# Latent attention: score rows of 640 keys split as 384 + 256 columns, and one query copy on ScalarE

## The chip, the cores and the metric

The kernel runs on one core of a Trainium2 chip. The metric is the device time of one execution in microseconds (us). An execution that the hardware profiler recorded shows for every engine when each instruction began and how long it took. The engines are TensorE (PE, with its weight loads as PEld), VectorE (DVE), ScalarE (ACT), GpSimd (POOL) and SyncE (SP, which here only issues DMAs). Each takes its instructions in the order of the program and waits on semaphores for the others.

## The reference

A trunk of two layers over 1024 tokens of width 1024: differential attention, then multi-head latent attention, each followed by a gated MLP with a short causal convolution; RMSNorm before each. The change touches the latent attention alone, which computes for 16 heads

```python
q = (c_q @ w_uq).reshape(b, s, 16, 64 + 32)           # 64 plain, 32 rotary
kv = (c_kv @ w_ukv).reshape(b, s, 16, 64 + 64)        # keys, values
sc = (q_nope . k_nope + q_pe . k_pe) * scale
p = softmax(where(key_chunk <= query_chunk, sc, -max))  # chunks of 64 tokens
o = p @ v
```

A block of 128 queries sees its own and all earlier keys, so query block i (0 to 7) needs (i + 1) x 128 columns of scores.

## The kernel before

Matmuls run in a rounded 32-bit format, three for one product: every operand is kept as a high part (a copy into that format) and a low part (the rest), and `mm3` adds high x low, high x high and low x high. Its three calls stand in the profile as lines L120, L121 and L122. High parts are made by `hi` (L126 when it goes to DVE, L128 on ACT), low parts by `lo` (L131, on DVE or POOL).

One step of the attention (`MlaStep`) takes one head and two neighbouring query blocks, j = 0 and 1:

- `scores(j)`: `mm3` into a tile S of PSUM (1024 columns, two banks; there are two such tiles, used in turn, so a score row can begin only when the row before the last has been read out). A matmul writes at most 512 columns, so a row is cut by `blocks(n)` into 512 and the rest. Then DVE writes the mask into a corner (L2017) and takes the row's maximum (L2018), and ACT takes the exponential with its sum (L2019; the sum is read out by a second ACT instruction on the same line), which frees the tile.
- `weigh(j)`: DVE inverts the sum (L2025), POOL scales the row (L150).
- `turn`: PE transposes the weighted rows by 128 columns into a bank b (L264; three banks in turn, shared with the projections of queries and keys), ACT and DVE make high and low parts of it, tiles u.
- `product`: those by the values, on L2039 and L2040; ACT and DVE add up the two halves (L2042, L2043) and ACT's queue stores them (L2045).

A row of 640 keys is query block i = 4: step p = 2, j = 0, once a head, 16 times in all. In `scores` the row begins at column 0 of its tile:

```python
sc, e = k.big()[:, :n], self.e[:, :n] if n > 512 else ...
for b, m in blocks(n):
    k.mm3(sc[:, b : b + m], q[:, 0, qs], ...)
```

Between the steps, the projections of the next pair of heads are woven in: `q_unit` projects 512 tokens of one head's queries by nine matmuls into a bank, DVE multiplies by the rotary table (L1720, into a tile h), and the high and low parts go into a tile s. Which engine makes each part is read from strings with one letter per call (S for ACT, V for DVE, P for POOL): `QUERIES` for the high and `QUERIES_LOW` for the low parts, at place 2 x head + half.

The order on each engine is not that of the code. A scheduler keeps the dependencies and, with its own estimates, chooses at each point what an engine issues next; only the differential attention has an order written by hand. So an edit of one instruction can move others after it.

Of the kernel before, what the change touches and what calls it, by code (L numbers as in the profile page):

```python
# [18 lines left out]
P = 128  # L19
# [21 lines left out]
def blocks(n, step=512):  # L41
    return [(a, min(step, n - a)) for a in range(0, n, step)]
# [14 lines left out]
class Trunk:  # L57
# [1608 lines left out]
    ROTARY = "SV"  # L1666
    VALUES = "SSVSSSSS"
    WEIGHTS = "SVSSSSSS"
    QUERIES = "SSSVSSSSSSSSSSSSSSSSSSSSSSSSSSSS"
    QUERIES_LOW = "VPPVPPVPPPPPPPPPPPPPPPPPPPPPPPPP"  # L1670
    KEYS = "SSSVSSSSSSSSSSSSSSSSSSSSSSSSSSSS"
    UNITS_AT = (2, 2, 3, 5, 5, 7)
# [1 line left out]
    def mla_heads(self, cT, v_d, o_d):  # L1674
# [33 lines left out]
        def q_unit(h, half):  # L1708
# [11 lines left out]
            nc.vector.tensor_mul(t, acc, cs[:, s])  # L1720
            self.hi(q[:, 0, s], t, eng(self.QUERIES[2 * h + half]))
            self.lo(q[:, 1, s], t, q[:, 0, s], eng(self.QUERIES_LOW[2 * h + half]))
# [106 lines left out]
class DaStep(Step):  # L1829
# [37 lines left out]
    def scores(self, j):  # L1867
        k, nc, hd = self.k, self.k.nc, self.hd
        i = 2 * self.p + j
        n = (i + 1) * P  # L1870
        q = hd["q"][i // 4]
        qs = slice((i % 4) * P, (i % 4 + 1) * P)
        sc = self.sc[j] = []
        for c in range(2):
            if c == 0 or not self.one:
                ps = k.big()
            sc.append(ps[:, c * 512 : c * 512 + n] if self.one else ps[:, :n])
        self.both[j] = ps.rearrange("p (c n) -> p c n", c=2)
        for b, m in blocks(n):
            kt = hd["k"][b // 512]  # L1880
            for x, (qp, kp) in enumerate(((1, 0), (0, 1), (0, 0))):
                for c in range(2):
                    rows = slice(64 * c, 64 * c + 64)
                    nc.tensor.matmul(sc[c][:, b : b + m], q[rows, qp, qs], kt[rows, kp, :m], start=x == 0, stop=x == 2)  # L1884
# [114 lines left out]
class MlaStep(Step):  # L1999
# [5 lines left out]
    def scores(self, j):  # L2005
        k, nc = self.k, self.k.nc
        i = 2 * self.p + j
        n = (i + 1) * P
        q, kt = self.hd["q"], self.hd["k"]
        qs = slice(i * P, (i + 1) * P)  # L2010
        nm, l = k.stat(), k.stat()
        if j == 0 or n > 512:
            self.e = self.R.P([P, S])
        sc, e = k.big()[:, :n], self.e[:, :n] if n > 512 else self.e[:, j * 512 : j * 512 + n]
        for b, m in blocks(n):
            k.mm3(sc[:, b : b + m], q[:, 0, qs], q[:, 1, qs], kt[:, 0, b : b + m], kt[:, 1, b : b + m], True, True)
        nc.vector.memset(sc[0:64, n - 64 : n], NEG)  # L2017
        nc.vector.tensor_reduce(nm, sc, axis=AX.X, op=ALU.max, negate=True)  # L2018
        nc.scalar.activation(e, sc, AF.Exp, bias=nm, accum_out=l)  # L2019
        self.l.append(l)  # L2020
        self.probs.append(e)
# [314 lines left out]
```

## Time and profile before

| | us |
|---|---|
| median of 3 runs (2372.78 to 2373.3) | 2373.1 |
| the profiled execution | 2372.74 |
| its span, first to last instruction | 2370.9 |
| PE busy | 2345.3 |
| DVE busy | 1919.9 |
| ACT busy | 1259.6 |
| POOL busy | 583.5 |

The granted clock of TensorE is 0.999. The latent attention's steps run from about 1285 to 1636 us of the span. A record of the timeline has start, length, engine, line, operation, output tile and input tiles with their sizes, and, in brackets, how long the engine was idle before it and what ended that. In the table of stretches a row has the stretch, its length, the busy time and count of PE, PEld, DVE, ACT and POOL, the granted clock, the DMA share and GB/s. A matmul's end is modelled, and matmuls overlap.

### The profile page before, as it was taken

The page shows a single profiled execution, that of the slowest core. Times are in us where ns is not written, and L with a number is a line of the kernel's source. Part 1 is how long each engine was busy: PE and PEld are TensorE (multiplying, and loading weights), DVE is VectorE, ACT ScalarE, POOL GpSimd, SP SyncE. Part 2 cuts the span into 40 slices and gives each one's busy share as a digit, 9 for nine tenths or more (in the row PEclk, how much of TensorE's full clock was granted, in tenths as well). Part 3 has the DMA queues.
Part 4 walks back from the last instruction along what each step waited for, and adds up shares of the span by engine and source line. Part 5 has one row for each costly group of instructions (what it writes and reads, how often), then busy time and mean ns, then how long its engine had stood idle before and what let it go on. Part 6 is the DMA issues. An engine that isn't in the chain of part 4 may idle for free.

```text
span 2370.9 us, 32976 instructions
## 1 busy us (share of the span) xinstructions
PE 2345.3 (99%) x12146; PEld 1976.2 (83%) x12146; DVE 1919.9 (81%) x3170; ACT 1259.6 (53%) x2315; POOL 583.5 (25%) x465
## 2 busy tenths in 40 slices
PE   9999999999999999999999999999999999999998
PEld 7888888788888888888898889988888888888886
DVE  6777878858888888999865888886588888889997
ACT  5666666745444444354444777775454444443444
POOL 4545444323000000000133666673420000000001
PEclk9999999999999999999999999999999999999999
DMA  3111111332222222652221211133322222227502
GB/s 148 40 36 36 49 37 54 111 134 94 89 80 81 80 89 80 234 174 86 84 99 56 72 33 39 41 98 110 114 79 88 80 80 83 87 80 284 178 1 80
DMA packets 95667, 213.42 MB, mean 90 GB/s; under 512 B 8713, under 2 KB 33937, under 8 KB 95505
## 3 DMA queue, kind: packets, MB, share of 16 engines
q1 hardware_dynamic: 86304, 183.51, 23.5%
q10 hardware_dynamic: 9200, 27.80, 3.2%
q8 instruction: 96, 1.57, 0.3%
q14 instruction: 67, 0.54, 0.1%
HBM read 158.85 MB, written 52.43 MB: 89 GB/s over the span
## 4 chain that ended last, share of the span: by engine, by line
PE 91%; DVE 5%; DMA 1%; ACT 1%; issue 1%; POOL 0%; POOLq 0%; DVEq 0%; SPq 0%; ACTq 0%
PE S L122 14%; PE S L120 14%; PE S L121 14%; PE b L120 9%; PE b L122 8%; PE b L121 8%; PE u L120 5%; PE u L122 5%; PE u L121 4%; PE S L1884 3%; PE b L264 2%; PE u L2040 1%; PE b L1930 1%; PE u L2039 1%; DVE s L131 1%
## 5 line engine op out<-in xcount | busy, mean ns | idle before, releaser
L168 POOL TENSOR_TENSOR st<-st,mhalf 128x1 f32<-128x1 f32 x56 | 35.3, 632 | 1296.1 <-DVE st L165 1287.4
L120 PE MATMUL S<-s,u 128*128 128x512 f32 (+1 forms) x800 | 301.8, 377 | 0.2 <-ACT u L1110 0.2
L122 PE MATMUL S<-s,u 128*128 128x512 f32 (+1 forms) x800 | 301.2, 376 | 0.1
L121 PE MATMUL S<-s,u 128*128 128x512 f32 (+1 forms) x800 | 301.0, 376 | 0.0
L128 ACT CAST u<-h 128x512 fp32r<-128x512 f32 (+1 forms) x194 | 115.8, 619 | 267.1 <-DVE h L1031 262.8
L120 PE MATMUL b<-s,u 128*128 128x512 f32 x588 | 230.8, 393 | 1.1 <-DVE u L131 0.4
L122 PE MATMUL b<-s,u 128*128 128x512 f32 x588 | 229.1, 390 | 0.0
L121 PE MATMUL b<-s,u 128*128 128x512 f32 x588 | 229.0, 389 | 0.0
L1088 DVE SCALAR_TENSOR_TENSOR u<-u,conv,u 128x1023 f32<-128x1023 f32 (+1 forms) x176 | 225.1, 1279 | 0.8 <-ACT u L1084 0.7
L150 POOL TENSOR_TENSOR u<-u,st 128x512 f32<-128x512 f32 (+7 forms) x160 | 173.1, 1090 | 161.1 <-DVE st L2025 107.3
L128 ACT CAST s<-u 128x512 fp32r<-128x512 f32 (+3 forms) x229 | 144.2, 663 | 100.2 <-PE u L122 28.7
L128 ACT CAST u<-b 128x512 fp32r<-128x512 f32 (+1 forms) x256 | 134.9, 547 | 92.1 <-PE b L1930 57.7
L131 DVE TENSOR_TENSOR u<-b,u 128x512 fp32r<-128x512 f32 (+1 forms) x256 | 158.6, 631 | 23.9 <-ACT u L128 22.8
L120 PEld LDWEIGHTS S<-s,u 128*128 128x128 f32 x800 | 150.6, 188 | 27.9 <-ACT u L1110 0.5
L122 PEld LDWEIGHTS S<-s,u 128*128 128x128 f32 x800 | 150.6, 188 | 27.8 <-DVE u L131 0.3
L121 PEld LDWEIGHTS S<-s,u 128*128 128x128 f32 x800 | 150.6, 188 | 27.4
L120 PE MATMUL u<-s,s 128*128 128x512 f32 (+1 forms) x408 | 165.1, 405 | 1.1 <-DVE s L131 0.9
L122 PE MATMUL u<-s,s 128*128 128x512 f32 (+1 forms) x408 | 158.3, 388 | 0.0
L121 PE MATMUL u<-s,s 128*128 128x512 f32 (+1 forms) x408 | 157.6, 386 | 0.0
L131 DVE TENSOR_TENSOR s<-u,s 128x512 fp32r<-128x512 f32 (+2 forms) x205 | 140.8, 721 | 15.0 <-ACT s L128 14.7
L1091 ACT ACTIVATE u<-u 128x1024 f32<-128x1024 f32 x44 | 46.7, 1062 | 187.4 <-DVE u L1088 187.4
L131 DVE TENSOR_TENSOR u<-h,u 128x512 fp32r<-128x512 f32 x171 | 118.1, 691 | 32.4 <-ACT u L128 31.5
(294 smaller groups left out, 6389.6 us busy)
## 6 DMA issues: line engine op xcount, KB each, us to landing
u<-in_ffn_up SPq DMA_DIRECT2D x88, 512.0 KB, 3.9
g_d<-u ACTq DMA_DIRECT2D x44, 512.0 KB, 2.6
u<-in_ffn_down SPq DMA_DIRECT2D x66, 256.0 KB, 4.7
u<-g_d SPq DMA_DIRECT2D x62, 256.0 KB, 4.1
s<-in_da_wqkv SPq DMA_DIRECT2D x23, 512.0 KB, 3.3
x_d<-u SPq DMA_DIRECT2D x16, 512.0 KB, 2.6
s<-x_d SPq DMA_DIRECT2D x8, 1024.0 KB, 10.5
s<-g_d SPq DMA_DIRECT2D x18, 256.0 KB, 5.3
```

The costliest lines, as they stand in the source:

```text
L120: mm(out, lh, rl, start=first, stop=False, skip_group_check=onto)
L121: mm(out, lh, rh, start=False, stop=False, skip_group_check=onto)
L122: mm(out, ll, rh, start=False, stop=last, skip_group_check=onto)
L128: self.nc.scalar.copy(out, src)
L131: (eng or self.nc.vector).tensor_sub(out, src, hi.bitcast(F32))
L150: self.nc.gpsimd.tensor_mul(x, x, s.to_broadcast(list(x.shape)))
L168: nc.gpsimd.tensor_tensor(r, s, self.mhalf, ALU.pow)
L264: self.nc.tensor.transpose(ps[:, j * P : (j + 1) * P], probs[t][:, k : k + P], self.ident)
L1088: nc.vector.scalar_tensor_tensor(t[half][:, back:], u[half][:, : S - back], w, t[half][:, back:], ALU.mult, ALU.add)
L1091: nc.scalar.activation(t[0], t[0], AF.Silu)
L1884: nc.tensor.matmul(sc[c][:, b : b + m], q[rows, qp, qs], kt[rows, kp, :m], start=x == 0, stop=x == 2)
L1930: k.nc.tensor.transpose(ps[:, j * P : (j + 1) * P], self.e[t][0][:, c : c + P], k.ident)
```

## The change

Two edits. The 640-column row is written from column 128 of its tile on (columns 128 to 767), and its matmuls are cut at 384, so that 384 columns lie in the tile's first bank and 256 in its second. And the one V in `QUERIES` becomes S: the high part for head 1, second half, is copied by ACT.

```diff
-    QUERIES = "SSSVSSSSSSSSSSSSSSSSSSSSSSSSSSSS"
+    QUERIES = "SSSSSSSSSSSSSSSSSSSSSSSSSSSSSSSS"
...
-        sc, e = k.big()[:, :n], self.e[:, :n] if n > 512 else self.e[:, j * 512 : j * 512 + n]
-        for b, m in blocks(n):
+        skip = P if n == 5 * P else 0
+        sc, e = k.big()[:, skip : skip + n], self.e[:, :n] if n > 512 else self.e[:, j * 512 : j * 512 + n]
+        for b, m in ((0, 3 * P), (3 * P, 2 * P)) if skip else blocks(n):
             k.mm3(sc[:, b : b + m], q[:, 0, qs], q[:, 1, qs], kt[:, 0, b : b + m], kt[:, 1, b : b + m], True, True)
```

In the changed kernel all lines from L2014 on have a number one higher. The scheduler also moves instructions: some 880 rows of PE's order differ, 420 of DVE's, 200 of ACT's and 60 of POOL's, none of SP's. Three places follow; an order row has line, operation, output, inputs and size, and the last number of a tile's name is the same in both kernels.

First DVE's order at the start of the steps, at the moved copy. S_12057 is a score row of 256 columns, s_1935_11778 the queries of head 1, h_1969_11996 its product with the table. Before:

```order
L1720 TENSOR_TENSOR h_1969_11996<-b_11986,u_1839_11126 128x512
L2017 MEMSET S_12057 64x64
L126 CAST s_1935_11778<-h_1969_11996 128x512
L2018 TENSOR_REDUCE st_1985_12055<-S_12057 128x1
L131 TENSOR_TENSOR s_1935_11778<-h_1969_11996,s_1935_11778 128x512
L2025 RECIPROCAL st_1986_12056<-st_1986_12056 128x1
```

Now:

```order
L1720 TENSOR_TENSOR h_1969_11996<-b_11986,u_1839_11126 128x512
L2018 MEMSET S_12057 64x64
L2019 TENSOR_REDUCE st_1985_12055<-S_12057 128x1
L131 TENSOR_TENSOR s_1935_11778<-h_1969_11996,s_1935_11778 128x512
L2026 RECIPROCAL st_1986_12056<-st_1986_12056 128x1
```

The copy (L126) has gone from between the mask and the maximum of S_12057.

ACT's order there, before:

```order
L128 CAST s_1860_11259<-u_12003 128x2x64
L128 CAST s_1921_11665<-h_1967_11982 128x512
L1613 COPY u_1970_12002<-u_12003 128x512
L2019 ACTIVATE u_1979_12030,st_1986_12056<-S_12057,st_1985_12055 128x256
L1613 COPY u_1970_12002<-b_12004 128x512
L128 COPY s_1916_11645<-u_1956_11932 32x2x512
```

Now:

```order
L128 CAST s_1921_11665<-h_1967_11982 128x512
L1613 COPY u_1970_12002<-u_12003 128x512
L128 CAST s_1935_11778<-h_1969_11996 128x512
L2020 ACTIVATE u_1979_12030,st_1986_12056<-S_12057,st_1985_12055 128x256
L1613 COPY u_1970_12002<-b_12004 128x512
L128 COPY s_1916_11645<-u_1956_11932 32x2x512
```

The copy (of h_1969_11996) stands directly ahead of the exponential of S_12057.

Then ACT's order in the middle of the stage, around a score row of 768 columns, S_14202. Tiles b are banks with transposes, s_2434 a query's high part, h_2444 an output's sum, u_2586 the high part of a weight. Before:

```order
L128 CAST u_2451_14111<-b_14107 128x384
L2019 ACTIVATE u_2461_14145,st_2460_14144<-S_14146,st_2459_14143 128x640
L2019 ACTIVATE u_2474_14201,st_2473_14200<-S_14202,st_2472_14199 128x768
L128 CAST u_2586_14706<-u_2558_14594 128x1024
L2042 COPY h_2444_14080<-u_14081 64x256
L128 CAST s_2434_14039<-h_2476_14212 128x512
L128 CAST u_2465_14171<-b_14166 128x512
L128 CAST u_2467_14179<-b_14174 128x512
```

Now:

```order
L128 CAST u_2586_14706<-u_2558_14594 128x1024
L2020 ACTIVATE u_2461_14145,st_2460_14144<-S_14146,st_2459_14143 128x640
L128 CAST s_2434_14039<-h_2476_14212 128x512
L2043 COPY h_2444_14080<-u_14081 64x256
L128 CAST u_2465_14171<-b_14166 128x512
L128 CAST u_2467_14179<-b_14174 128x512
L2020 ACTIVATE u_2474_14201,st_2473_14200<-S_14202,st_2472_14199 128x768
L128 CAST u_2469_14187<-b_14182 128x512
```

The exponential of S_14202 stood right behind that of S_14146 and ahead of the copies of the banks b_14166 and b_14174. Now it stands behind them. The same holds for six more of these rows, S_13635, S_13912, S_14479, S_14769, S_15046 and S_15336; an eighth, S_15613, stands behind a weight's copy and an output copy.

Last PE's order at the same place. S_14282 is the next-but-one score row after S_14202 and takes the same tile. Before, behind the last matmul of S_14202:

```order
L122 MATMUL S_14202<-s_1976_12027,s_2305_13472 128x256
L264 MATMUL b_14107<-ident,u_2432_14031 128x128 x3
L2039 MATMUL u_14081<-u_2437_14055,s_2283_13381 128x256
L2040 MATMUL u_14081<-u_2437_14055,s_2283_13381 128x256
L2039 MATMUL u_14081<-u_2437_14055,s_2283_13381 128x256
L2040 MATMUL u_14081<-u_2437_14055,s_2283_13381 128x256
L120 MATMUL b_14156<-s_1904_11597,u_2328_13572 128x512
L121 MATMUL b_14156<-s_1904_11597,u_2328_13572 128x512
L122 MATMUL b_14156<-s_1904_11597,u_2329_13573 128x512
L120 MATMUL b_14156<-s_1904_11597,u_2328_13572 128x512
L121 MATMUL b_14156<-s_1904_11597,u_2328_13572 128x512
L122 MATMUL b_14156<-s_1904_11597,u_2329_13573 128x512
```

S_14241 and S_14282 follow further on, S_14282 thirty rows behind S_14202. Now, up to the first matmul of S_14282:

```order
L264 MATMUL b_14174<-ident,u_2454_14118 128x128
L264 MATMUL b_14182<-ident,u_2454_14118 128x128
L264 MATMUL b_14182<-ident,u_2448_14096 128x128
L264 MATMUL b_14182<-ident,u_2454_14118 128x128
L2040 MATMUL u_14129<-u_2451_14111,s_2283_13381 128x256
L2041 MATMUL u_14129<-u_2451_14111,s_2283_13381 128x256
L2040 MATMUL u_14129<-u_2451_14111,s_2283_13381 128x128
L2041 MATMUL u_14129<-u_2451_14111,s_2283_13381 128x128
L264 MATMUL b_14190<-ident,u_2448_14096 128x128
L264 MATMUL b_14190<-ident,u_2454_14118 128x128 x2
L120 MATMUL S_14282<-s_1916_11645,s_2395_13865 128x512
```

S_14202 has moved to behind the first transposes of b_14166 and b_14174, S_14282 to behind all transposes of its neighbours; between the last transpose of b_14174 and S_14282 stand six transposes and four products.

## The prediction

> **What bounds the kernel now.** I read the page first, then the busy times by stretch, then the timeline of the latent attention, the one stage that the change touches.
>
> ```profile
> span 2370.9 us, 32976 instructions
> PE 2345.3 (99%) x12146; PEld 1976.2 (83%) x12146; DVE 1919.9 (81%) x3170; ACT 1259.6 (53%) x2315; POOL 583.5 (25%) x465
> PE 91%; DVE 5%; DMA 1%; ACT 1%; issue 1%; POOL 0%; POOLq 0%; DVEq 0%; SPq 0%; ACTq 0%
> ```
>
> PE bounds the whole: 91% of the chain that ended last is its work. So time is won where PE gets less to do or waits less, and lost where it waits more. The busy times by stretch (PE, PEld, DVE, ACT, POOL in that order) of the latent attention:
>
> ```profile
> 1285.00:1325.00 40.00, 37.42 (x201) 30.48 (x200) 33.02 (x74) 30.03 (x68) 25.61 (x20) 1.00 0.35 109
> 1421.50:1463.00 41.50, 41.50 (x274) 37.53 (x274) 34.38 (x85) 32.11 (x71) 27.80 (x22) 1.00 0.13 39
> 1546.00:1590.00 44.00, 42.95 (x275) 37.89 (x274) 36.39 (x88) 34.29 (x75) 26.95 (x22) 1.00 0.22 68
> 1590.00:1636.00 46.00, 44.82 (x310) 40.51 (x310) 39.01 (x93) 36.07 (x78) 27.81 (x23) 1.00 0.38 120
> ```
>
> PE idles 2.6 us in the start, 1.1 and 1.2 us in the last two stretches, and nothing in the middle, where two heads take 41.5 us. There PE's record overlaps itself (a 512-column matmul stands for 0.39 us, the next begins 0.23 us later), so I read starts, not busy time. DVE is at 83% in the middle: little air.
>
> **Part 1, the columns.** Sixteen times, once a head, three matmuls of 512 and three of 128 columns become three of 384 and three of 256. Starts in PE's timeline:
>
> ```profile
> 1391.48 0.34 PE L120 MATMUL S<-s,s 128*128 128x384 f32 x1
> ...
> 1392.02 0.49 PE L264 MATMUL b<-ident,u 128*128 128x128 f32 x3
> ...
> 1393.05 0.39 PE L120 MATMUL S<-s,s 128*128 128x512 f32 x1
> ...
> 1393.74 0.39 PE L120 MATMUL b<-s,u 128*128 128x512 f32 x1
> ...
> 1397.94 0.22 PE L120 MATMUL S<-s,s 128*128 128x128 f32 x1
> ...
> 1398.22 0.45 PE L120 MATMUL S<-s,s 128*128 128x512 f32 x1
> ...
> 1398.97 0.28 PE L120 MATMUL S<-s,s 128*128 128x256 f32 x1
> ...
> 1399.32 0.49 PE L264 MATMUL b<-ident,u 128*128 128x128 f32 x3
> ```
>
> Each pair of rows brackets three matmuls: 0.54 us for 384 columns, 0.69 for 512, 0.28 for 128, 0.35 for 256. Before 0.69 + 0.28 = 0.97, after 0.54 + 0.35 = 0.89; 16 x 0.08 = 1.3 us less on the bounding engine. The 128 columns cost too much for their size: 0.28 is over a third of 0.69, not a quarter. The shift by 128 columns changes no count: still 640 columns over one bank border for DVE's maximum and ACT's exponential, so 0.
>
> The Trainium skill (TensorE: Matmul & The Clock Gate, Back-to-back issue gap) gives an isolated matmul a gap of N/2.4 + 2.5 ns, by which both splits take the same and the gain is an estimated 0; its sustained figure for N=128, 81 ns instead, lies nearer to these rows, which I follow. By the isolated rule the sum below would be 1.3 us higher.
>
> **Part 2, the copy.** One high part of queries (first pair, second head, second half) goes from DVE to ACT.
>
> ```profile
> 1299.82 0.62 ACT L128 CAST s<-h 128x512 fp32r<-128x512 f32 x1 [0.23 <-DVE h L1720]
> 1301.50 0.11 DVE L2017 MEMSET S<- 64x64 f32 x1
> 1301.53 2.49 DVE L126 CAST s<-h 128x512 fp32r<-128x512 f32 x1
> ...
> 1302.92 0.82 PE L264 MATMUL b<-ident,u 128*128 128x128 f32 x6
> ...
> 1303.94 0.41 DVE L2018 TENSOR_REDUCE st<-S 128x1 f32<-128x256 f32 x1
> 1304.39 0.47 ACT L2019 ACTIVATE u<-S,st 128x256 f32<-128x256 f32 x1 [2.93 <-DVE st L2018]
> 1304.76 0.19 ACT L2019 ACTIVATION_READ_ACCUMULATOR u<-S,st 128x1 f32 x1
> ...
> 1305.00 0.50 PE L120 MATMUL S<-s,s 128*128 128x512 f32 x1 [1.26 <-ACT u L2019]
> ```
>
> This is the longest wait of PE in the stage. The copy holds DVE for 2.49 us, the maximum behind it is late, the exponential too, and PE cannot have the score buffer. Six transposes at 0.11 us (a group of four stands for 0.62, of three for 0.52, below) end their issue at 1302.92 + 0.65 = 1303.57; PE starts at 1305.00: 1.43 us lost, and 0.1 on restarting. On ACT the copy costs 0.62, in an idle time of 2.93. Queued behind it there is this same exponential: the maximum could now end at 1302.1, the copy at about the same time, the exponential at 1302.8, before PE comes. So -1.5 us, the whole wait. Bounds: 0 if another wait stands right behind it, -2.6 if all idle time of the first stretch goes. I take -1.5, since the rows name DVE as the one cause.
>
> **Part 3, the moved order.** The scheduler, given these two edits, writes all four compute queues anew from there; SP's queue keeps its order. That is the largest term. In the middle, the score row of 768 columns now comes after the first transposes of the step before it, and its exponential stands on ACT behind two copies of those transposes (the pieces under the change). The next-but-one score row needs the same buffer. What such a chain takes, in today's rows with a 384-column exponential in its place:
>
> ```profile
> 1465.35 0.28 PE L2040 MATMUL u<-u,s 128*128 128x128 f32 x1
> 1465.46 0.62 PE L264 MATMUL b<-ident,u 128*128 128x128 f32 x4
> ...
> 1467.58 0.60 PE L264 MATMUL b<-ident,u 128*128 128x128 f32 x4
> 1467.94 0.36 PE L2039 MATMUL u<-u,s 128*128 128x256 f32 x1
> ...
> 1468.32 0.28 PE L2040 MATMUL u<-u,s 128*128 128x128 f32 x1
> 1468.60 0.52 PE L264 MATMUL b<-ident,u 128*128 128x128 f32 x3
> 1468.87 0.31 PE L120 MATMUL S<-s,s 128*128 128x128 f32 x1
> 1469.02 0.27 PE L121 MATMUL S<-s,s 128*128 128x128 f32 x1
> ```
>
> ```profile
> 1467.14 1.08 ACT L128 CAST u<-b 128x512 fp32r<-128x512 f32 x2
> 1468.10 0.60 ACT L2019 ACTIVATE u<-S,st 128x384 f32<-128x384 f32 x1
> 1468.58 0.21 ACT L2019 ACTIVATION_READ_ACCUMULATOR u<-S,st 128x1 f32 x1
> ```
>
> Two copies, the exponential, its accumulator read, ending at 1468.79; PE starts the row that takes the buffer at 1468.87. The same release with 768 columns is in the start:
>
> ```profile
> 1317.89 2.37 POOL L131 TENSOR_TENSOR u<-u,u 128x1024 fp32r<-128x1024 f32 x1
> ...
> 1319.03 0.91 ACT L2019 ACTIVATE u<-S,st 128x768 f32<-128x768 f32 x1
> ...
> 1319.83 0.19 ACT L2019 ACTIVATION_READ_ACCUMULATOR u<-S,st 128x1 f32 x1
> ...
> 1320.07 0.50 PE L120 MATMUL S<-s,s 128*128 128x512 f32 x1
> ```
>
> From the exponential's start to the accumulator's end 0.99 us, and PE 0.05 later. Now the new chain, counted from the point at which PE has issued the last transpose of the second bank. Its result is there 0.24 later (the group at 1467.58 ends at 1468.18, its successor starts at 1467.94) and ACT begins some 0.06 after that: 0.30. The first copy began three transposes (0.33) earlier, at -0.03, and ends at 0.51; the second ends at 1.05; the exponential overlaps it by 0.12 and is read out at 1.92; PE may start at 1.98. In the new order PE has for this time three transposes, four products and three transposes: 0.33 + 0.41 + 0.33 = 1.07 us (0.11 a transpose; the four products are 1468.32 - 1467.94 and the 0.11 of 1465.35 to 1465.46, less the 0.08 that a restart after transposes adds). So PE waits 0.9 us. The order has eight such rows (seven behind two copies, one behind other ACT work): 8 x 0.9 = +7.2 us. Bounds: 0 each if the casts run ahead of my count, 1.5 each by the rival below. I keep 0.9, since every piece of it is a row and today's order shows the same release at 0.08.
>
> Against it: today's wait in the middle goes, four times once per two heads. The transposes at 1468.60 start 0.28 after their forerunner, where 0.11 is the rule (1465.35 to 1465.46): 0.17; the matmuls after them start 0.15 late in all (1468.87 to 1469.02 is 0.15, not 0.06, and two more steps alike). 4 x 0.32 = -1.3. What else is moved is covered: the output store on ACT's queue goes behind one more copy, and its data is wanted only by the next projection; POOL takes low parts (2.37 us for 1024 columns, above) ahead of a scaling of the 1024-column row, and is busy for 27.80 of 41.5 us. Were that cover gone, each such place costs PE what POOL is late, which I bound by the rival's 0.6. In the last 50 us the order changes as well; I put 0, bounded by today's idle time there, -2.3 if it all went and +2.3 if it doubled.
>
> **The sum.** The profiled execution took 2372.74 us, 1.84 around its span of 2370.9; the median of the three runs, 2373.1, is 0.36 above. From 2372.7: -1.3 - 1.5 + 7.2 - 1.3 = +3.1, so 2375.8 by this execution, 2376.2 by the median; I say 2376.0. Inside the 0.2% (4.7 us) that a measurement of this kernel can tell from no change, on the slow side.
>
> **Rivals.**
> - *Slower by more: DVE comes late at the same eight places.* Rows of DVE: maximum of 384 columns 0.54, a low part 0.69. If DVE does both maxima before the low part of the first bank, the transposes of the fourth bank (three exist) wait for that: some 0.6 us beyond the 0.9. For it: 83% busy in the middle, and a POOL queue that now puts a low part ahead. Against it: DVE has 7.1 us of idle time in the 41.5. It decides once DVE's low part ends later than ACT's exponential. 8 x 1.5 - 4.1 = +7.9: 2380.6.
> - *The moved rows are hidden:* ACT has the copies done early, the eight waits are nothing, today's wait stays: -1.3 - 1.5 = -2.8, so 2370. For it: ACT is at 77% there, and today's chain costs PE hardly 0.1. Against it: the count above.
> - *Faster:* hidden as well, and the start loses all its idle time of 2.6, today's middle wait goes: -1.3 - 2.6 - 1.3 = -5.2, 2367.5. For it: DVE gets back up to 2.49 us in the start, and three engines are late there. Against it: only 1.43 of the 2.6 has a row that leads to the copy.
>
> **How the numbers follow.** Forecast 0.46, DVE late 0.26, hidden 0.20, faster 0.08. Slower by over 0.2% (above 2377.8): the DVE case less a little, and the upper end of the forecast: 0.34. Faster (below 2368.4): 0.09. Same: 0.57. The likeliest case alone spans 2373.5 to 2378.5 (0.6 to 1.2 a place). The range takes in "hidden" and most of "DVE late": 2369.5 to 2381.0.
>
> **What would show it.** Right: no PE wait at the score row after 1302.9 and an exponential there that ends near 1302.8; three-matmul blocks of 0.54 and 0.35 in the 640-column rows; in the middle, about 0.9 us before the row that follows each 768-column row's pair, released by ACT's exponential, two heads in some 42.8 us (41.5 + 1.8 - 0.3 - 0.2) instead of 41.5. Wrong: two heads in 41 us (the waits are hidden), or in 44 (DVE), with DVE's low part named as releaser of the transposes.

## The result, and the profile after

The changed kernel takes 2381.37 us in the median of six runs (2380.12 to 2382.25), beside 2372.94 (2370.96 to 2374.68) for the kernel before: a ratio of 1.0036, 95% interval 1.0025 to 1.0047. It is slower by 8.4 us. The forecast of 2376.0 and the range up to 2381.0 were both too low. The profiled execution took 2381.71.

The page of the kernel after: the span, the busy times, and the chain that ended last.

```profile
span 2379.9 us, 32945 instructions
PE 2348.3 (99%) x12146; PEld 1977.3 (83%) x12146; DVE 1920.5 (81%) x3169; ACT 1259.4 (53%) x2316; POOL 583.5 (25%) x465
PE 89%; DVE 6%; ACT 2%; issue 1%; POOL 1%; DMA 1%; DVEq 0%; POOLq 0%; ACTq 0%; SPq 0%
```

No engine got more work. PE's part of the chain fell from 91 to 89%, while DVE's and ACT's grew: PE waits more. Where, is in the busy times by stretch (PE, PEld, DVE, ACT, POOL, then the granted clock):

```profile
1285.00:1325.00 40.00, 38.47 (x204) 30.91 (x203) 32.74 (x77) 31.18 (x71) 26.62 (x20) 1.00 0.36 109
1427.19:1470.69 43.50, 42.22 (x273) 37.70 (x273) 34.63 (x85) 31.91 (x71) 28.03 (x23) 1.00 0.13 37
1557.69:1597.00 39.31, 37.07 (x232) 33.34 (x233) 31.75 (x75) 29.58 (x64) 22.85 (x20) 0.96 0.18 50
```

The start has more PE work in the same 40 us than before. The middle repeats every 43.5 us where it took 41.5, with nearly the same busy time on DVE, ACT and POOL. And one late stretch has a granted clock of 0.96.

To see where the lag arises I took the start of the same projection matmul (L120, into a bank b from a slot s) in both traces:

| start before | start after | after less before | what lies between this row and the last |
|---|---|---|---|
| 1287.24 | 1286.94 | -0.3 | other stages |
| 1305.57 | 1303.69 | -1.9 | the copy on ACT |
| 1328.87 | 1327.78 | -1.1 | the rest of the start |
| 1343.66 | 1342.44 | -1.2 | |
| 1386.22 | 1385.92 | -0.3 | the place at 1385: the new cycle begins |
| 1427.76 | 1428.64 | +0.9 | two heads |
| 1469.30 | 1472.14 | +2.8 | two heads |
| 1510.84 | 1515.71 | +4.9 | two heads |
| 1552.13 | 1559.28 | +7.2 | two heads |
| 1573.07 | 1584.11 | +11.0 | the place at 1580 |
| 1640.11 | 1649.12 | +9.0 | the last 60 us (a product, L2039 before, L2040 after) |

So 8.4 us are lost bit by bit from 1343 to 1552. The row before the last overstates its place. In all other rows PE has as many instructions behind it in both kernels, to within three. At 1584.11 it has eight more behind it (8445) than at 1573.07 before (8437). By the steps of the rows (0.23 us for 512 columns, 0.12 for 256, 0.11 for a transpose) that is an estimated 1.1 us more work done since the row above. For equal work some 2.8 of the 3.9 us are lost at that place, and some 1.1 of the 2.0 come back after it.

**The start**, in the timeline of the kernel after:

```profile
1301.25 0.62 ACT L128 CAST s<-h 128x512 fp32r<-128x512 f32 x1
1301.37 0.42 DVE L2019 TENSOR_REDUCE st<-S 128x1 f32<-128x256 f32 x1
1301.83 0.47 ACT L2020 ACTIVATE u<-S,st 128x256 f32<-128x256 f32 x1
...
1302.58 0.82 PE L264 MATMUL b<-ident,u 128*128 128x128 f32 x6
1303.15 0.47 PE L120 MATMUL S<-s,s 128*128 128x512 f32 x1
```

The copy takes 0.62 on ACT, the exponential ends at 1302.30, and the score row follows its transposes with no wait.

**The row of 768 columns**, which the prediction turned on:

```profile
1446.51 1.25 PE L264 MATMUL b<-ident,u 128*128 128x128 f32 x10
1446.59 0.96 DVE L2019 TENSOR_REDUCE st<-S 128x1 f32<-128x768 f32 x1
1447.20 1.07 ACT L128 CAST u<-b 128x512 fp32r<-128x512 f32 x2 [1.22 <-PE b L264]
...
1447.76 0.56 DVE L2019 TENSOR_REDUCE st<-S 128x1 f32<-128x384 f32 x1
...
1447.90 0.28 PE L2041 MATMUL u<-u,s 128*128 128x128 f32 x1
...
1448.16 0.92 ACT L2020 ACTIVATE u<-S,st 128x768 f32<-128x768 f32 x1
1448.24 1.28 DVE L131 TENSOR_TENSOR u<-b,u 128x512 fp32r<-128x512 f32 x2
1448.96 0.21 ACT L2020 ACTIVATION_READ_ACCUMULATOR u<-S,st 128x1 f32 x1
1448.97 0.55 PE L264 MATMUL b<-ident,u 128*128 128x128 f32 x3 [0.80 <-DVE u L131]
...
1449.28 0.47 PE L120 MATMUL S<-s,s 128*128 128x512 f32 x1
```

Ten transposes stand in a row and fill all three banks. The first bank comes free only when DVE's low part of it ends (1448.93), and that low part stands behind both maxima. The last product before them started at 1447.90, so PE loses 0.96 us, and 0.06 in restarting. ACT's exponential is read out at 1449.17, just before PE is there for the buffer (1449.28). In every second head the order on DVE is milder, and PE loses 0.35 at the transposes and 0.28 at the score row, each with a restart: 0.78 in all. Ahead of these three places (1426, 1470 and 1513) a product also starts 0.21 late.

**The row of 640 columns**, a place for which the sum had no term, in the kernel after and, in the second fence, before:

```profile
1439.05 1.20 DVE L2019 TENSOR_REDUCE st<-S 128x1 f32<-128x1024 f32 x1
...
1440.18 0.67 DVE L131 TENSOR_TENSOR u<-b,u 128x512 fp32r<-128x512 f32 x1
...
1440.63 0.28 PE L122 MATMUL S<-s,s 128*128 128x256 f32 x1
...
1440.88 0.69 DVE L131 TENSOR_TENSOR s<-b,s 64x512 fp32r<-64x512 f32 x1
1441.00 0.52 PE L264 MATMUL b<-ident,u 128*128 128x128 f32 x3
...
1441.63 0.50 PE L120 MATMUL b<-s,u 128*128 128x512 f32 x1
```

```profile
1439.22 0.69 DVE L131 TENSOR_TENSOR u<-b,u 128x512 fp32r<-128x512 f32 x1 [0.32 <-ACT u L128]
1439.94 0.69 DVE L131 TENSOR_TENSOR s<-b,s 64x512 fp32r<-64x512 f32 x1
...
1440.85 0.49 PE L264 MATMUL b<-ident,u 128*128 128x128 f32 x3
1441.09 0.48 PE L120 MATMUL b<-s,u 128*128 128x512 f32 x1
```

The transposes start 0.37 after the last score matmul, where 0.12 is usual, and the projection behind them waits too. Each starts right behind one of DVE's two low parts, which now stand behind the maximum of 1024 columns; before, both were done when PE came. Counted from start to start, with the restarts, it is 0.67 us, at 1441, 1484 and 1528, once in two heads. At 1400 the projection alone waits as long, for a low part behind the maximum of 640 columns.

**The place at 1385**, where the new cycle begins, had no term for a loss either:

```profile
1384.72 0.52 PE L264 MATMUL b<-ident,u 128*128 128x128 f32 x3 [0.54 <-DVE u L131]
1385.45 0.33 PE L120 MATMUL S<-s,s 128*128 128x128 f32 x1 [0.21 <-ACT u L2020]
```

From the last product to the projection PE takes 2.01 us here (1383.91 to 1385.92) and took 0.98 before (1385.24 to 1386.22), with the same instructions. The exponential that the score row waits for stands behind three copies on ACT instead of two.

**The place at 1580**: the eighth of the rows of 768 columns.

```profile
1577.69 1.05 ACT L128 CAST s<-u 128x1024 fp32r<-128x1024 f32 x1 [1.88 <-DMA u<-in_mla_w_o]
...
1579.04 0.90 ACT L2020 ACTIVATE u<-S,st 128x768 f32<-128x768 f32 x1
...
1580.08 0.53 PE L120 MATMUL S<-s,s 128*128 128x512 f32 x1 [1.85 <-ACT u L2020]
```

```profile
1577.00:1580.40 3.40, 1.55 (x13) 1.29 (x12) 2.56 (x6) 2.68 (x6) 1.64 (x2) 1.00 0.04 14
1580.41:1583.82 3.41, 3.41 (x15) 2.86 (x14) 2.97 (x7) 2.89 (x8) 2.24 (x2) 0.50 0.60 192
```

ACT waits 1.88 us for a weight's transfer with the exponential queued behind the weight's copy. PE waits 1.85 for that exponential, and then its clock is halved for 3.41 us.

### The profile page after: what moved, and what is told of

The parts are those of the page before. It is cut to its first block, busy times and chain, and to the rows that moved or that the text cites. A ratio compares the mean times of both kernels' runs of the same rounds, so it can differ in the third digit from the quotient of the medians.

```text
span 2379.9 us, 32945 instructions
## 1 busy us (share of the span) xinstructions
PE 2348.3 (99%) x12146; PEld 1977.3 (83%) x12146; DVE 1920.5 (81%) x3169; ACT 1259.4 (53%) x2316; POOL 583.5 (25%) x465
## 4 chain that ended last, share of the span: by engine, by line
PE 89%; DVE 6%; ACT 2%; issue 1%; POOL 1%; DMA 1%; DVEq 0%; POOLq 0%; ACTq 0%; SPq 0%
PE S L120 13%; PE S L122 13%; PE S L121 13%; PE b L120 9%; PE b L121 8%; PE b L122 8%; PE u L120 5%; PE u L122 4%; PE u L121 4%; PE S L1884 3%; PE b L264 2%; PE b L1930 1%; PE u L2041 1%; DVE s L131 1%; PE u L2040 1%
## 5 line engine op out<-in xcount | busy, mean ns | idle before, releaser
L120 PE MATMUL S<-s,u 128*128 128x512 f32 (+1 forms) x800 | 301.7, 377 | 0.2 <-ACT u L1110 0.2
L120 PE MATMUL b<-s,u 128*128 128x512 f32 x588 | 230.5, 392 | 1.2 <-DVE s L131 0.7
L120 PEld LDWEIGHTS S<-s,u 128*128 128x128 f32 x800 | 150.5, 188 | 27.9 <-ACT u L1110 0.5
L120 PE MATMUL u<-s,s 128*128 128x512 f32 (+1 forms) x408 | 165.1, 405 | 1.1 <-DVE s L131 0.9
```

The costliest lines, as they stand in the source:

```text
L120: mm(out, lh, rl, start=first, stop=False, skip_group_check=onto)
```

## The experiments

Theory: the columns and the copy are each worth what the rows said, and the loss lies in the new order that the scheduler writes. Rivals: the copy burdens ACT; or score rows of 384 and 256 columns from column 128 on are themselves slower. Three facts made a clean test possible. The copy alone leaves every queue as it was, but for the one moved instruction. The columns alone bring about the whole new order. And an order can be held, whatever the scheduler would do, by links that only fix the order of issue:

```diff
+PINNED = {"PE": "...", "DVE": "...", ...}     # instructions in the wanted order
+def pin(tc):
+    now = {i.name: i for i in tc.nc.cur_bb.bb.instructions}
...
+            if behind:
+                tc.add_manual_dep(i, behind, mybir.DependencyInfo(mybir.DependencyClass.NoSync, ...))
         kernel_body(tc, aps, out)
+        pin(tc)
```

All runs in one table. "Two heads" is the mean over four heads of the middle, "1343 to 1552" the time between two projection matmuls that bound it in the kernel before; both are from the traces. Traces enter this stage up to 2.5 us apart (1285.1 to 1287.6) with the same code ahead of it, so differences of that size are read from these columns, not from the medians.

| run | median us | ratio to before, 95% | two heads | 1343 to 1552 |
|---|---|---|---|---|
| before | 2372.0 to 2372.9 | | 41.54 | 208.5 |
| changed kernel | 2381.37 | 1.0025 to 1.0047 | 43.54 | 216.8 |
| copy_alone | 2371.42 | 0.9989 to 1.0007 | 41.57 | 208.6 |
| columns_alone | 2382.55 | 1.0031 to 1.0059 | 43.53 | 216.8 |
| both_old_order | 2370.41 | 0.9981 to 0.9999 | 41.41 | 207.8 |
| order_alone | 2383.11 | 1.0033 to 1.0058 | 43.70 | 217.6 |
| old_order_30 | 2380.17 | 1.0020 to 1.0045 | 43.11 | 215.3 |
| old_order_50 | 2379.06 | 1.0017 to 1.0039 | 42.50 | 213.8 |
| old_order_80 | 2373.32 | 0.9996 to 1.0013 | 42.08 | 210.5 |
| low_earlier | 2381.35 | 1.0023 to 1.0052 | 43.51 | 216.6 |
| exp_earlier | 2381.82 | 1.0025 to 1.0054 | 43.57 | 216.8 |
| both_earlier | 2381.03 | 1.0025 to 1.0051 | 43.56 | 216.8 |
| weight_later | 2385.05 | 1.0036 to 1.0066 | 43.56 | 216.9 |
| both_weights_later | 2381.62 | 1.0026 to 1.0060 | 43.54 | 216.8 |
| bank_first | 2379.69 | 1.0020 to 1.0042 | 43.29 | 216.2 |
| place_640 | 2383.55 | 1.0031 to 1.0061 | 44.09 | 218.4 |
| bank_first_640 | 2380.84 | 1.0024 to 1.0052 | 43.51 | 216.7 |
| bank_exp | 2380.78 | 1.0021 to 1.0047 | 43.27 | 215.7 |
| bank_exp_add | 2378.67 | 1.0017 to 1.0037 | 42.97 | 214.8 |

### Edits and order taken apart

**copy_alone**

```diff
-    QUERIES = "SSSVSSSSSSSSSSSSSSSSSSSSSSSSSSSS"
+    QUERIES = "SSSSSSSSSSSSSSSSSSSSSSSSSSSSSSSS"
```

> Only the copy of the one high part of queries goes from DVE to ACT; the columns stay as before. No queue changes its order but for that one instruction. Theory (the loss of the changed kernel comes from the new order of the queues, which the columns bring about): 1.5 us faster than before, 2371.4, the wait of PE at 1305 gone and the middle as before (41.5 us for two heads). Rival A (the copy burdens ACT and makes its exponentials late): slower, 2375 or more, with two heads in over 42 us.

**columns_alone**

```diff
+        skip = P if n == 5 * P else 0
-        sc, e = k.big()[:, :n], ...
+        sc, e = k.big()[:, skip : skip + n], ...
-        for b, m in blocks(n):
+        for b, m in ((0, 3 * P), (3 * P, 2 * P)) if skip else blocks(n):
```

> Only the columns change (384 and 256 from column 128 on); the copy stays on DVE. The queues stand as in the changed kernel but for the copy. Theory (order): the loss of the changed kernel plus the 1.5 us that the copy saves, 8.4 + 1.5 = 9.9 us over before, 2382.8, two heads in 43.5 us. Rival A (copy): about 1.3 us faster than before, 2371.6.

**both_old_order**: both edits, and the links hold PE, DVE, ACT and POOL to the order of copy_alone.

```diff
+        pin(tc)      # PINNED: the order of copy_alone
```

> Both edits, but every engine is held to the order of the kernel before (the moved copy excepted) by issue-order links. Theory (order): nothing of the loss is left and both gains stand, -1.3 - 1.5 = -2.8 us, 2370.1; two heads in 41.5 - 0.16 = 41.3 us. Rival C (the score rows themselves are slower as 384 and 256 columns from column 128 on, or DVE and ACT read them more slowly there): it keeps most of the loss, 2379 or more, two heads in over 43 us.

**order_alone**: the kernel before, and the links hold it to the order of columns_alone.

```diff
+        pin(tc)      # PINNED: the order of columns_alone
```

> Neither edit: the matmuls and engines of the kernel before, held to the order that the columns bring about (that of the run with the columns alone). Theory (order): the loss of columns_alone without the 1.3 us that the columns save, so 9.9 us over before or up to 1.3 more, 2382.8 to 2384.1, two heads in 43.5 us. Rival C (columns): as before, 2373, two heads in 41.5 us.

The theory holds in all four. The copy by itself is worth little (2371.42 beside 2371.98, within the interval), the columns by themselves cost all of it (2382.55), the new order without any edit costs as much (2383.11), and both edits in the old order make the fastest kernel of all, 2370.41. The traces show that the orders were held: on PE, DVE, ACT and POOL the rows of both_old_order stand as in copy_alone, those of order_alone as in columns_alone. This is the page and the middle of both_old_order:

```profile
span 2368.5 us, 32976 instructions
1425.00:1466.40 41.40, 41.26 (x274) 37.54 (x273) 34.49 (x84) 32.21 (x71) 27.81 (x23) 1.00 0.14 39
```

Both rivals fall: ACT does the copy in copy_alone with two heads in 41.57, and the 384 and 256 columns stand in both_old_order with two heads in 41.41. The columns' own price comes out twice: 41.57 - 41.41 = 0.16 in the old order, 43.70 - 43.53 = 0.17 in the new one, 0.08 a head. The Trainium skill (TensorE: Matmul & The Clock Gate, Back-to-back issue gap) would have given an estimated 0 by its isolated rule; the runs decide for the rows.

### A rate, or one event

**old_order_30, old_order_50, old_order_80**: both edits, PE alone held to the old order, and only for the first 30, 50 or 80% of the stretch in which the orders differ.

```diff
-PINNED = {"PE": "...", "DVE": "...", "Activation": "...", "Pool": "..."}
+PINNED = {"PE": "..."}     # the first 30 (50, 80)% of PE's list
```

> Both edits; only PE is held, and only for the first 30% of the stretch in which the orders differ, to the order of the kernel before; the rest is left to the scheduler, which falls back into the new cycle from the eighth head on. Theory (each head in the new cycle costs about 1.1 us, (2381.4 - 2370.4 - 1.9 for the place at 1580) / 8; the loss is a rate, not one event): 5.5 heads are left in it, 2370.4 + 1.9 + 5.5 x 1.1 = 2378.3. Rival (the loss comes from the way into the new cycle, once, or from the last stretch): 2381 as the changed kernel, or 2372.

> As old_order_30, but PE is held for the first 50%: the scheduler falls back into the new cycle from the tenth head on. Theory (a rate): 3.5 heads are left in it, 2370.4 + 1.9 + 3.5 x 1.1 = 2376.1. Rival (one event): the same time as old_order_30.

> As old_order_30, but PE is held for the first 80%, and the scheduler then keeps to the old order of PE to the end by itself; DVE and ACT differ from it in a few places. Theory (a rate): nothing of the loss is left, 2370.4, as with all engines held. Rival (DVE's and ACT's order count by themselves): 2372 or more.

The stretch from 1343 to 1552 falls from 216.8 by steps to 215.3, 213.8 and 210.5: a rate, as the theory had it. Let go at 30 or 50%, the scheduler falls back into the new cycle; let go at 80%, it keeps PE's old order to the end. But each run took 2 to 3 us more than expected, and old_order_80 shows why. There PE has the old order to the end, two heads take 42.08 and not 41.41, and the rival about DVE's order is right. DVE in old_order_80 and, in the second fence, in both_old_order, with PE's transposes:

```profile
1425.69 0.69 DVE L2019 TENSOR_REDUCE st<-S 128x1 f32<-128x512 f32 x1
...
1426.30 1.28 DVE L131 TENSOR_TENSOR u<-b,u 128x512 fp32r<-128x512 f32 x2
...
1427.13 0.52 PE L264 MATMUL b<-ident,u 128*128 128x128 f32 x3 [0.88 <-DVE u L131]
```

```profile
1425.03 0.69 DVE L131 TENSOR_TENSOR u<-b,u 128x512 fp32r<-128x512 f32 x1 [0.25 <-ACT u L128]
...
1425.87 0.52 PE L264 MATMUL b<-ident,u 128*128 128x128 f32 x3
...
1426.34 0.67 DVE L2019 TENSOR_REDUCE st<-S 128x1 f32<-128x512 f32 x1
```

A maximum of 512 columns that stands ahead of the low part of the first bank costs PE 1.05 us there instead of 0.31, once in two heads.

### What in the new order waits

The next runs hold the changed kernel to its own order with single rows moved.

**low_earlier** (four places)

```diff
 DVE: maximum of 768
+DVE: low part of the first bank
 DVE: mask, maximum of 384
-DVE: low part of the first bank
```

> The changed kernel, held to its own order, but in four places of the middle (PE waits there at 1449, 1492, 1536 and 1559 for DVE's low part) the low part of the first bank stands on DVE ahead of the maximum of 384 columns. Theory 1 (DVE alone sets the wait): each place gets back what the low part gains, 0.55 us (the maximum's duration), 4 x 0.55 = -2.2 us, 2379.2. Theory 2 (ACT is as late: the exponential of 768 columns is read out at 1449.17 and PE starts the row that needs its buffer at 1449.28): the wait only passes from the transposes to the score row behind them, at most 4 x 0.1 = -0.4 us, 2381.0.

**exp_earlier** (seven places)

```diff
 ACT: copy of the first bank
+ACT: exponential of 768
 ACT: copy of the second bank
-ACT: exponential of 768
```

> The changed kernel, held to its own order, but in seven places of the middle the exponential of 768 columns stands on ACT between the two copies of transposed banks, not behind both. Theory 1 (ACT's exponential behind two copies is what costs): up to 7 x 0.5 = -3.5 us, 2377.9. Theory 2 (both engines are late at once): the four places where DVE's low part stands behind both maxima keep their wait of 0.8 to 1.0 us, the other three lose their 0.28 before the score row, -0.8 us, 2380.6; the second copy comes 0.9 later, which can give that back (2381.4).

**both_earlier**: both moves.

> Both moves together: DVE's low part ahead of the maximum of 384 columns in four places, ACT's exponential between the two copies in seven. Theory 2 (both engines are late at once): more than the two alone add up to; the score row can start at 1448.85 instead of 1449.28 in four places, and loses 0.28 in three: 4 x 0.43 + 3 x 0.28 = -2.6 us, 2378.8. Rival (the order of PE itself leaves too little work between the two rows, so that what one of these engines gains the other lacks): within 1 us of the changed kernel, 2380.4 or more.

Nothing is won by any of the three: two heads stay at 43.5 to 43.6. The waits only change places. In low_earlier:

```profile
1448.28 0.55 PE L264 MATMUL b<-ident,u 128*128 128x128 f32 x3 [0.39 <-DVE u L131]
...
1448.66 0.21 ACT L2020 ACTIVATION_READ_ACCUMULATOR u<-S,st 128x1 f32 x1
...
1448.93 0.50 PE L120 MATMUL S<-s,s 128*128 128x512 f32 x1
```

The wait at the transposes falls from 0.96 to 0.56, and 0.27 and a restart of 0.1 appear at the score row, which waits for ACT. Theory 2 is right for low_earlier. For both_earlier it promised 2.6 us, and the rival was right: 0.56 at the transposes stays, since copy and low part of the first bank need that time, and 0.29 comes at the next projection's bank, whose copy is now late.

**bank_first** (seven places, with low_earlier's move on DVE)

```diff
 PE: score row of 768
+PE: the other transposes of the first bank
 PE: score row of 384
-PE: the other transposes of the first bank
 PE: transposes of the second and third bank
```

> The changed kernel, held to its own order, but in the seven places of the middle PE finishes the transposes of the first bank ahead of the score row of 384 columns instead of behind it (and, as in low_earlier, DVE's low part of that bank stands ahead of the maximum of 384 columns in four of them). Theory 3 (PE's order is what makes ACT and DVE late: ten transposes in a row, the first copy begins 1.2 us after ACT went idle): the copy starts 0.54 earlier, the wait at the fourth bank falls from 1.0 and 0.4 to 0.3 or less, the score row behind it is then bound by the exponential: 0.4 to 0.5 a place, 7 x 0.45 = -3.2 us, two heads in 42.6, 2378.2. Rival (ACT and DVE simply have too much work between the two score rows): the wait moves to the score row as in low_earlier, two heads in 43.3 or more, 2380.7 or more.

**place_640** (three places)

```diff
+DVE: low part of a bank, low part of a key
 DVE: maximum of 1024
-DVE: low part of a bank, low part of a key
```

> The changed kernel, held to its own order, but in three places (PE waits there at 1441, 1484 and 1528) the low parts of a transposed bank and of a key stand on DVE ahead of the maximum of 1024 columns instead of behind it. Theory (the 0.67 us that PE loses there in every two heads is DVE's, held up by that maximum): 3 x 0.67 = -2.0 us, two heads in 42.9, 2379.4. Rival (the maximum, and with it the exponential of 1024 columns and POOL's scaling, come late instead and PE waits at the next row): within 0.5 us of the changed kernel, 2380.9 or more, two heads in 43.4 or more.

**bank_first_640**: both moves.

> Both moves. If they are independent they add up: -3.2 - 2.0 = -5.2 us, two heads in 42.0, 2376.2. If the waits only move on to the next place that needs DVE or ACT: less than the larger of the two alone, 2379 or more, two heads in 42.8 or more.

In bank_first the wait for the fourth bank is gone in every second head, and its place is taken by the exponential behind two copies, the very wait that the prediction had counted:

```profile
1446.68 0.52 PE L264 MATMUL b<-ident,u 128*128 128x128 f32 x3
...
1447.36 0.20 ACT L2020 ACTIVATION_READ_ACCUMULATOR u<-S,st 128x1 f32 x1
...
1447.62 0.50 PE L120 MATMUL S<-s,s 128*128 128x512 f32 x1 [0.43 <-ACT u L2020]
```

Two heads take 43.29: 0.25 won, where theory 3 had 0.9 and the rival at most 0.2. place_640 lost time: the wait at 1441 shrinks by 0.19, but the maxima behind come later, and the wait at the row of 768 columns grows from 0.96 to 1.70. Two heads take 44.09. So the two places are tied together by DVE's queue: a row moved ahead at one makes the other wait longer. bank_first_640 ends at 43.51; the two do not add up.

**bank_exp**: bank_first and the move of exp_earlier. **bank_exp_add**: also, in four places:

```diff
-DVE: addition of an output (waits for ACT's copy of it)
 DVE: mask, maximum of 768
+DVE: addition of an output
```

> bank_first, and ACT's exponential of 768 columns stands between the two copies of transposed banks in the seven places (as in exp_earlier). If the positions must all be right at once: the wait of 0.59 us before the score row in every second place goes and the small ones shrink, two heads in 42.7 instead of 43.3, about 2378. Rival (too little time whatever stands first): a wait of 0.3 us or more at the next bank, as in exp_earlier, two heads in 43.1 or more, 2379.2 or more.

> bank_exp, and in four places DVE's addition of an output, which waits 1.0 us for ACT, comes behind the maximum of 768 columns instead of ahead of it. If the positions must all be right at once: maximum and exponential come 0.4 earlier there, a further 0.2 to 0.4 in every two heads, 42.4, about 2377. Rival (too little time): as bank_exp within 0.1 per two heads.

bank_exp stays at 43.27, with 0.41 at the next projection's bank: the rival. bank_exp_add gets to 42.97. So positions on PE, ACT and DVE moved together win back 0.57 of the 2.0 us, DVE's addition that waits 1.0 us for ACT being half of it. 42.4 was expected. What the rest of the cycle would need, other than the old order, stays open.

### The place at 1580

**weight_later**

```diff
-ACT: high part of a weight of the output projection (1024 columns)
 ACT: exponential of 768, two copies, exponential of 384, a copy
+ACT: high part of that weight
```

and its low part on DVE likewise.

> The changed kernel, held to its own order, but the split of one weight of the output projection (high part on ACT, low part on DVE), which waits for its transfer at 1577.69 ahead of the exponential of 768 columns, comes behind the exponential of the next row, some 4 us later. Theory (the wait of 2.0 us at 1580 is the transfer's, through ACT's queue, and PE then runs slowly for 3 us, about 1.8 us more): the wait falls to 0.9 or less and the slow stretch is gone, -1.1 - 1.8 = -2.9 us, 2378.5. Rival (the last stretch only takes the time back in other waits: PE catches up 2 us there as it is): -0.9 us or less, 2380.5.

The wait at 1580 falls to 0.63 us, as expected, but nothing is won: the median is 2385.05 beside 2381.37 (the intervals of the two ratios overlap), and from 1343 to the stage's end the trace is 2.1 us longer than the changed kernel's. The raw buffer of this weight comes free later, so the next weight's transfer starts later, and the same thing happens 10 us further on, to another exponential:

```profile
1587.50 1.04 ACT L128 CAST s<-u 128x1024 fp32r<-128x1024 f32 x1 [4.31 <-DMA u<-in_mla_w_o]
...
1588.95 0.50 PE L120 MATMUL S<-s,s 128*128 128x512 f32 x1 [2.10 <-ACT u L2020]
```

**both_weights_later**: the second weight's high and low part also move, behind the split of the weight after it.

```diff
-ACT: high part of the next weight in that buffer
 ACT: ... copy of the weight after it, exponential of 896, a query's copy
+ACT: high part of the next weight in that buffer
```

> The changed kernel, held to its own order, but the splits of two weights of the output projection that share one raw buffer come later on ACT and DVE (the first behind the exponential of the next row, as in weight_later, the second behind the split of the weight after it, some 8 us later), so that neither waits for its transfer ahead of an exponential that PE waits for. Theory (at 1580 PE waits for a transfer through ACT's queue and then runs at half clock): the wait falls from 2.0 us to the 0.63 that weight_later shows there, nothing of 2 us follows, no half clock in the stage; 2.0 - 0.6 + 1.1 to 1.7 for the clock = 2.5 to 3.1 us less at 1590, and of it at least 0.5 is left at the end: 2378.3 to 2380.9. Rival (such a wait only moves on to the next place that needs the same queue): a wait of 1 us or more elsewhere before 1610, and 2381 or more.

Now no wait of 2 us and no half clock is left in the stage, and the projection that started at 1584 starts 2.6 us earlier, as the theory had it. But three waits between 1596 and 1601 (0.44, 0.30 and 0.77 us), which the changed kernel doesn't have, take 1.5 of it back, the largest released by DVE's addition (L2044); some 0.5 is left at the stage's end, and the median (2381.62) shows nothing. On the end result the rival was right, though the single wait of 1 us that it named did not come: time won at 1580 is waited for again behind it. Why the stretch behind it gives the time back in either kernel stays open.

## Why the prediction was right or wrong

- **The columns, -1.3: right.** 0.08 a head, in the old order and in the new.
- **The copy, -1.5 at its place: right there, half of it given back.** The wait at 1305 is gone and 1.6 us are won by 1304; 0.8 of it go again by 1328, in waits that stood behind, for a low part on POOL (1305.27) and a high part on DVE (1305.91) among others. The bound "0 if another wait stands right behind it" was nearer than I took it. In copy_alone, counted from the entry of the stage, the lag also goes from -1.6 to -0.9 within this stretch.
- **The eight places, +7.2 at 0.9 each: the size right for seven of them, in part by luck, since the reason was not, and the eighth mis-sized.** PE loses 1.02 and 0.78 us by turns, 0.90 in the mean. But the wait is first for DVE's low part behind both maxima, which I had put down as a rival with a chance of 0.26, and ACT's exponential is ready at the same moment. The rival added the two up to 1.5; low_earlier and bank_first show that they overlap: without the one, PE waits for the other.
- **"What else is moved is covered", 0: this is the step that failed.** Between 1343 and 1552 PE loses 0.67 us at each of four places at the score rows ahead of a projection (1400, 1441, 1484, 1528), where DVE's low parts now stand behind a maximum. At 1385, where the sum had a gain of 0.3, it loses 1.0. Three products start 0.21 late. Together that is some 4.6 us against the sum, a little more than the stretch lacks. By the sum's own terms, seven places less the old wait and the columns, the stretch should have grown by 6.3 - 1.3 - 0.8 = 4.2; it grew by 8.4. I had followed the new order at the row of 768 columns only.
- **The eighth place, 0.9 in the sum: some 2.8 by 1584.** In the main these are the wait of 1.85 and about 1.1 for the half clock (below). The order showed a weight's copy ahead of this exponential, and I priced it as one more ACT instruction. Its operand comes by a transfer that can start only when another weight has left the raw buffer, and behind a wait of nearly 2 us PE ran at half clock.
- **The last 50 us, 0: some -1.1.** Within the bounds of 2.3 that stood there. In both_weights_later, which loses less at 1580, this stretch takes 2.1 us longer than in the changed kernel (from 1579.60 to 1646.73, beside 1584.11 to 1649.12). So it is the 1580 place taken back rather than a better order.

Together, from the entry of the stage to 1640: -0.9 in the start, +8.4 to 1552, some +2.8 at the eighth place and -1.1 behind it make 9.2, where the traces have 9.3 (-0.3 at the entry, +9.0 at 1640). Over half of what the forecast lacks lies in the places not followed. Of the signs named in advance, the two that pointed to "wrong" came true: two heads near 44 (43.5), with DVE's low part as releaser of the transposes.

## What to carry to other kernels

Where a scheduler writes the order, an edit has two prices, that of its own work and that of the order it brings about; here they are some -1.6 us (both_old_order, 2370.41 beside 2371.98) and some +11 us (order_alone, 2383.11 beside 2371.98), so take them apart by holding the order before judging the edit. When reading a moved order, follow each engine through one whole period and count what stands ahead of the instruction that frees a buffer, at every row and not only at the one that changed most. And a buffer can be late on two engines at once, as here: a move on one of them changed the name of the wait and hardly its length.

## What the runs showed of the hardware

A wait of PE of under 2 us can halve its clock for 3.41 us. In the changed kernel it followed an idle time of 1.85 us (the rows above). Whether it follows is not settled by the length alone: exp_earlier, with a wait of 1.76 us, kept its clock, bank_first and bank_exp with 1.99 too, and old_order_30, with 1.70, lost it.

The traces differ in where the wait lies. In each of the 19 the record of the granted clock drops only after a whole number of stretches of 3.413 us, counted from its first entry; in the changed kernel it is 461 of them, 1573.54 us. Up to 2355 us of the span there are nine drops, and in the stretch just ahead of each PE was idle for 1.85 to 2.22 us in all; in no other stretch was it idle for more than 1.58. At the program's end a stretch of the changed kernel with 1.90 us (from 2368.9) was followed by no drop, so the limit is not sharp in these records. No run moved the wait alone. In the fences PE's busy time is the first number behind the length. In exp_earlier a border at 1577.91 cuts the wait, so that 0.70 and 1.30 us of idle time fall into two stretches; in old_order_30 all 1.91 us fall into one:

```profile
1578.97 0.50 PE L120 MATMUL S<-s,s 128*128 128x512 f32 x1 [1.76 <-ACT u L2020]
1574.50:1577.91 3.41, 2.71 (x22) 2.40 (x20) 2.19 (x6) 1.60 (x3) 3.11 (x3) 1.00 0.41 139
1577.91:1581.32 3.41, 2.11 (x14) 1.63 (x14) 3.27 (x7) 3.38 (x8) 1.47 (x1) 1.00 0.41 72
```

```profile
1577.24 0.53 PE L120 MATMUL S<-s,s 128*128 128x512 f32 x1 [1.70 <-ACT u L2020]
1575.16:1578.57 3.41, 1.50 (x8) 0.76 (x7) 2.67 (x7) 3.39 (x8) 1.67 (x2) 1.00 0.17 17
1578.57:1581.98 3.41, 3.41 (x16) 3.31 (x17) 2.69 (x8) 2.65 (x7) 2.34 (x3) 0.50 0.53 180
```

The same place in exp_earlier cost 1.1 us less than in the changed kernel, so that is about what the half clock takes. The Trainium skill (TensorE: Matmul & The Clock Gate, Part 1: The HAM clock gate) describes a window of 3413 ns that runs freely and a half rate after an idle one. The length and the fixed borders agree with the traces; but a whole idle window, as the page has it, was not needed here.
